# Fixed order for the last branch product and the gated merge of a decoder trunk, with one weight split per block

## Chip, core and metric

The kernel runs on one core of a Trainium2 chip. Its time is the device time of one execution in microseconds; several executions are measured and the median is given. Lower is better.

## What is computed

The reference is one layer of a hybrid decoder trunk over 1024 tokens of width 1024. Three branches (a linear recurrence, a stick-breaking attention and a cross-attention) each give 512 columns per token. The part that matters here joins them:

```
branch_out = einsum('btnc,ncd->btnd', ys, w_branch)
gates = sigmoid(gate_logits)
merged = sum(gates * branch_out, axis=2)
x = x + merged @ w_out
x = x + conv_ffn(x, norm2_g, w_up, conv_w, conv_b, w_down)
```

## The kernel before

Matrix products are made in split form. An operand x is kept as a high part, a rounded copy of x in a format that TensorE multiplies directly, and a low part, x minus that copy. A product is then three matmuls: high by high, high by low, low by high. Splitting takes two steps. For a weight, ScalarE makes the high part (L80) and POOL the low part (L81), both in `split_raw`; `load_w` (L76) issues the load on SP's queue into one of two buffers named wr. A buffer can be loaded again only when POOL has finished with it.

Two of the three branches are done and summed when `branch_last` (L1259) starts. It treats the remaining branch, branch 0, in eight blocks d of 128 output columns, each over all 1024 tokens. One load of branch weights (named wr, split into wh and wl) serves two blocks. For each block:

- SP loads the block's gate (L1270, into g, a tile of the pool "at") and the sum of the other two branches (L1271, into o, a tile of the pool "w4"). Three blocks of each fit.
- TensorE makes 24 matmuls of 128 rows by 512 columns (L115) into two PSUM banks, pp[0] and pp[1], one for each half of the tokens. There are four banks of this kind ("mm"), so that block d + 2 writes the banks of block d.
- VectorE multiplies the banks by the gate (L1286, one PSUM and one SBUF input) and adds the other branches' sum (L1287, two SBUF inputs).
- ScalarE makes the high part of the result (L1293: one piece of 512 columns, two of 256) and VectorE the low part (L1294, two SBUF inputs). These are the tiles mg of the projection.

Beside this the output weights are split. `load_wo` (L1254) does it for one of eight weights k. Weights 0 to 3 go into tiles "qk", 4 to 6 into tiles "at", 7 into "it" and "sp". In the program text four of them are asked for in `branch_last`, at blocks 2 to 5, and four at the head of `out_proj` (L1296). The projection multiplies tile by tile: in its first round, rows 0 and 1 of the tokens take turns, six matmuls each, for k from 0 to 7.

The program text doesn't fix the order on an engine. A scheduler places each instruction by its dependences and priorities, except those that are handed to `keep_in_program_order`, which keep their order on their engine. Matmuls in this part are not pinned, and neither were the splits, copies and merge steps.

Of the kernel before, what the change touches and what calls it, by code (L numbers as in the profile page):

```python
# [11 lines left out]
F32 = mybir.dt.float32  # L12
F32R = mybir.dt.float32r
BF16 = mybir.dt.bfloat16
AF = mybir.ActivationFunctionType
ALU = mybir.AluOpType
# [33 lines left out]
class Trunk:  # L50
# [25 lines left out]
        self.nc.sync.dma_start(raw, src)  # L76
        return raw

    def split_raw(self, raw, hi, lo):
        self.nc.scalar.activation(hi, raw, AF.Copy)  # L80
        self.nc.gpsimd.tensor_tensor(lo, raw, hi.bitcast(F32), ALU.subtract)  # L81
        return hi, lo

    def split_w(self, src):
        raw = self.load_w(src)
        hi = self.pool_wt.tile([128, 1024], F32R, name=self.nm("wh"), tag="wh", bufs=2)
        lo = self.pool_wt.tile([128, 1024], F32R, name=self.nm("wl"), tag="wl", bufs=2)
        return self.split_raw(raw, hi, lo)

    def mm3(self, outs, w, x, first, last):  # L90
        for pi, (a, b) in enumerate(((0, 0), (0, 1), (1, 0))):
# [1159 lines left out]
            items.append(self.branch_item(b, d, st, first))  # L1251
        return load, hooks, items

    def load_wo(self, k):  # L1254
        slots = ["qk"] * 8 + ["at"] * 6 + ["it", "sp"]
        hl = [self.pool_l.tile([128, 1024], F32R, name="wo_sp", tag="sp", bufs=1) if s == "sp" else self.t4(s, F32R) for s in slots[2 * k : 2 * k + 2]]
        self.wo.append(self.split_raw(self.load_w(self.I["w_out"][k]), *hl))

    def branch_last(self):  # L1259
        nc = self.nc  # L1260
        self.wo = []
        y = self.split_y(self.yT, True)
        mg = lambda name, shape: self.pool_l.tile(shape, F32R, name=name, tag="l4")
        self.mg0 = [[mg(f"mg0_{i}_{k}", [128, 2, 512]) for k in range(4)] for i in range(2)]
        self.mg1 = [[[mg(f"mg1_{i}_{t}_{k}", [128, 4, 256]) for k in range(2)] for t in range(2)] for i in range(2)]
        for d in range(8):
            if d % 2 == 0:
                w = self.split_w(self.I["w_br"][0, d // 2])
            g, o = self.t4("at"), self.t4()
            nc.sync.dma_start(g, self.gsd[0, d])  # L1270
            nc.sync.dma_start(o, self.mrd[d])  # L1271
            pp = [self.ps("mm"), self.ps("mm")]
            if d == 0:
                for i, (a, b) in enumerate(((0, 0), (1, 0), (0, 1))):
                    for k in range(4):
                        for h in range(2):
                            self.mmul(pp[h], w[a][:, k * 256 : k * 256 + 128], y[k][b][:, h * 512 : (h + 1) * 512],
                                      start=(i == 0 and k == 0), stop=(i == 2 and k == 3))
            else:
                for k in range(4):  # L1280
                    self.branch_mm(d, w, y, pp, k)
            if d in (2, 3, 4, 5):
                self.load_wo(d - 2)
            for h in range(2):
                hs = slice(h * 512, (h + 1) * 512)
                nc.vector.tensor_tensor(g[:, hs], pp[h], g[:, hs], ALU.mult)  # L1286
                nc.vector.tensor_tensor(g[:, hs], g[:, hs], o[:, hs], ALU.add)  # L1287
                if h == 0:
                    parts = [[self.mg0[i][d // 2][:, d % 2] for i in range(2)] + [slice(0, 512)]]
                else:  # L1290
                    parts = [[self.mg1[i][t][d // 4][:, d % 4] for i in range(2)] + [slice(512 + 256 * t, 768 + 256 * t)] for t in range(2)]
                for hi, lo, ts in parts:
                    nc.scalar.activation(hi, g[:, ts], AF.Copy)  # L1293
                    nc.vector.tensor_tensor(lo, g[:, ts], hi.bitcast(F32), ALU.subtract)  # L1294

    def out_proj(self):  # L1296
        nc = self.nc
# [738 lines left out]
```

## Time and profile before

| | us |
|---|---|
| median of 3 executions | 1805.65 (1805.49 to 1806.79) |
| the profiled execution | 1808.55 |
| its span, first to last instruction | 1806.8 |
| TensorE busy in the span | 1783.4 |
| VectorE, ScalarE, POOL busy | 1182.9, 864.3, 791.7 |
| first matmul of block 0 | at 1018.47 |
| first matmul of the projection | at 1064.80 |

Times in rows of a timeline are microseconds from the start of the span: start, duration, engine, line, operation, output and inputs, number of instructions that the row joins, and in brackets the idle time before it with what ended it. A row of waits gives who waited, for whom, the total, how often, and the longest. A row of a line's instructions gives the shortest, median and longest duration in ns. A row of loads ends with their size and the median time from issue to landing. A row of a window gives its length, then busy time and number of instructions of TensorE, its weight loads, VectorE, ScalarE and POOL, the granted TensorE clock, the DMA share and GB/s. PE is TensorE, PEld its weight loads, DVE VectorE, ACT ScalarE, POOL GpSimd, SP the engine whose queue issues most loads.

### The profile page before, as it was taken

What the parts mean: (1) busy time and instruction counts of PE and PEld (TensorE: products, weight loads), DVE (VectorE), ACT (ScalarE), POOL (GpSimd) and SP (SyncE); (2) the same over time, 40 slices, a digit from 0 to 9 for tenths busy, and PEclk for the clock granted to TensorE, in tenths of its full rate; (3) what the DMA queues carried; (4) which work ended last, traced back from release to release, by engine and by line L of the source; (5) the groups of instructions that cost most, each with busy time, mean ns of one, the idle gap of its engine ahead of it and who ended that gap; (6) DMA issues with size and microseconds to landing.
All of it is one profiled execution on the core that took longest, in us unless ns stands there. A gap on an engine that the chain in (4) does not pass through costs nothing.

```text
span 1806.8 us, 27325 instructions
## 1 busy us (share of the span) xinstructions
PE 1783.4 (99%) x10479; PEld 1446.0 (80%) x10479; DVE 1182.9 (65%) x1626; ACT 864.3 (48%) x1556; POOL 791.7 (44%) x448
## 2 busy tenths in 40 slices
PE   9999999999999999999999999989999999999999
PEld 7777778888888888777777878867888888888887
DVE  5667775898987534244443872577776777795596
ACT  6444344566566535534444334543544444454343
POOL 3223353322231462122333542486767767545454
PEclk9999999999999999999999999999999999999999
DMA  5255664211112352577654553222332323486476
GB/s 208 59 163 176 196 208 157 73 42 45 53 56 88 115 129 79 192 239 277 206 187 176 186 198 106 105 87 88 123 100 88 116 101 111 134 304 226 146 237 206
DMA packets 122772, 261.29 MB, mean 145 GB/s; under 512 B 28681, under 2 KB 43657, under 8 KB 122514
## 3 DMA queue, kind: packets, MB, share of 16 engines
q1 hardware_dynamic: 85026, 193.83, 32.7%
q10 hardware_dynamic: 33840, 53.10, 8.0%
q0 software_dynamic: 3776, 12.62, 2.3%
q8 instruction: 82, 1.34, 0.3%
q14 instruction: 48, 0.39, 0.1%
HBM read 178.99 MB, written 80.48 MB: 144 GB/s over the span
## 4 chain that ended last, share of the span: by engine, by line
PE 69%; DVE 7%; ACT 3%; issue 2%; POOL 2%; DMA 1%; SPq 0%; DVEq 0%; POOLq 0%; ACTq 0%
PE mm L115 57%; PE g L115 10%; PE g L105 2%; DVE at L926 1%; DVE it L545 1%; DMA wr<-in_w_out_dram 1%; DVE mg L1294 1%; POOL wl L81 1%; DVE inst L547 1%; DMA A<-yd 0%; ACT at L1143 0%; DVE w L821 0%; DVE at L1286 0%; DVE g L1530 0%; DVE at L1287 0%
## 5 line engine op out<-in xcount | busy, mean ns | idle before, releaser
L81 POOL TENSOR_TENSOR wl<-wr,wh 128x1024 fp32r<-128x1024 f32 (+2 forms) x78 | 195.9, 2512 | 501.5 <-ACT wh L80 492.0
L115 PE MATMUL mm<-xhi,wh 128*128 128x512 f32 x784 | 260.1, 413 | 0.5 <-DVE w L322 0.4
L115 PE MATMUL mm<-xlo,wh 128*128 128x512 f32 x784 | 243.5, 392 | 0.0
L115 PE MATMUL mm<-xhi,wl 128*128 128x512 f32 x784 | 242.5, 391 | 0.0
L115 PEld LDWEIGHTS mm<-xlo,wh 128*128 128x128 f32 x784 | 147.1, 188 | 33.2 <-DVE xlo L199 0.3
L115 PEld LDWEIGHTS mm<-xhi,wl 128*128 128x128 f32 x784 | 147.0, 188 | 33.0 <-POOL wl L81 0.7
L115 PEld LDWEIGHTS mm<-xhi,wh 128*128 128x128 f32 x784 | 136.7, 190 | 29.2 <-issue 6.1
L80 ACT ACTIVATE wh<-wr 128x1024 fp32r<-128x1024 f32 (+2 forms) x78 | 81.8, 1048 | 146.4 <-PE mm L115 93.3
L115 PE MATMUL mm<-dw,da 128*128 128x512 f32 x528 | 121.0, 390 | 0.0
L115 PE MATMUL mm<-BT,wh 128*128 128x512 f32 x352 | 111.8, 399 | 6.7 <-DVE u L1585 5.8
L115 PE MATMUL mm<-BT,l 128*128 128x512 f32 x504 | 117.6, 389 | 0.0
L115 PEld LDWEIGHTS mm<-dw,da 128*128 128x128 f32 x528 | 98.9, 188 | 21.5 <-DVE da L1746 1.0
L1747 POOL TENSOR_TENSOR dw<-draw,dw 128x512 fp32r<-128x512 f32 x55 | 81.9, 1497 | 77.3 <-ACT dw L1745 75.9
L926 DVE TENSOR_TENSOR_SCAN at<-at,nrt 128x128 f32<-128x128 f32 (+3 forms) x64 | 94.2, 1479 | 25.5 <-ACT at L920 25.3
L115 PEld LDWEIGHTS mm<-BT,l 128*128 128x128 f32 x504 | 94.6, 188 | 19.7
L115 PE MATMUL mm<-B,wh 128*128 128x512 f32 x352 | 108.6, 390 | 0.0
L1746 DVE TENSOR_TENSOR da<-draw,da 128x512 fp32r<-128x512 f32 x77 | 65.9, 862 | 53.2 <-ACT da L1744 52.9
L1465 POOL TENSOR_TENSOR l<-it,l 128x1024 fp32r<-128x1024 f32 x21 | 51.2, 2436 | 92.9 <-ACT l L1462 92.8
L115 PE MATMUL g<-dw,da 128*128 128x512 f32 x396 | 90.2, 389 | 0.0
L821 DVE TENSOR_TENSOR w<-w,nrt 128x1024 f32<-128x1024 f32 x24 | 49.9, 2078 | 58.1 <-ACT w L820 47.1
L115 PEld LDWEIGHTS g<-dw,da 128*128 128x128 f32 x396 | 74.3, 188 | 15.4
L1744 ACT ACTIVATE da<-draw 128x512 fp32r<-128x512 f32 x77 | 48.1, 627 | 80.4 <-PE mm L115 32.3
(335 smaller groups left out, 3990.9 us busy)
## 6 DMA issues: line engine op xcount, KB each, us to landing
wr<-in_w_in_dram SPq DMA_DIRECT2D x48, 512.0 KB, 3.6
draw<-actd SPq DMA_DIRECT2D x77, 256.0 KB, 3.3
draw<-in_w_down_dram SPq DMA_DIRECT2D x55, 256.0 KB, 4.5
at<-scr SPq DMA_DIRECT2D x24, 512.0 KB, 5.8
wr<-in_w_up_dram SPq DMA_DIRECT2D x22, 512.0 KB, 3.5
actd<-gall ACTq DMA_DIRECT2D x44, 256.0 KB, 3.3
rw<-in_w_up_dram SPq DMA_DIRECT2D x20, 512.0 KB, 3.7
gsd<-w ACTq DMA_DIRECT2D x18, 512.0 KB, 2.8
```

Of the source, the lines that this page charges most:

```text
L80: self.nc.scalar.activation(hi, raw, AF.Copy)
L81: self.nc.gpsimd.tensor_tensor(lo, raw, hi.bitcast(F32), ALU.subtract)
L105: self.pinned(self.nc.tensor.transpose(out, in_, self.ident[:n, :n]))
L115: self.pinned(self.nc.tensor.matmul(*a, **k))
L545: self.pinned(nc.vector.tensor_tensor(tv, X[:, 0:s, s : s + 1].to_broadcast([128, s, n]), X[:, s : s + 1, s + 1 : 64].to_broadcast([128, s ...
L547: self.pinned(nc.vector.tensor_tensor(X[:, 0:s, s + 1 : 64], X[:, 0:s, s + 1 : 64], tv, ALU.add))
L821: nc.vector.tensor_tensor(g, g, self.nrb, ALU.mult)
L926: self.pinned(nc.vector.tensor_tensor_scan(sn[:, :W][:, ::-1], sn[:, :W][:, ::-1], self.nrt[:, 1152 - W :][:, ::-1], 1.0, ALU.mult, ALU.max))
L1465: ins = nc.gpsimd.tensor_tensor(lo, src, hi.bitcast(F32), ALU.subtract)
L1744: self.pinned(nc.scalar.activation(A[:, 0], a, AF.Copy))
L1746: self.pinned(nc.vector.tensor_tensor(A[:, 1], a, A[:, 0].bitcast(F32), ALU.subtract))
L1747: nc.gpsimd.tensor_tensor(Wt[:, 1], w, Wt[:, 0].bitcast(F32), ALU.subtract)
```

## The change

`split_raw`, `split_w` and `load_wo` take an argument `fix`, which by default does nothing. In `branch_last` it is `keep_in_program_order`. The merge steps of VectorE and ScalarE are pinned with it, and so are the splits that the loop asks for. The first two branch weights and output weight 0 are asked for ahead of the loop, unpinned. In the loop each of blocks 0 to 4 asks for one split, behind its merge: output weight 1, branch weight 2, output weight 2, branch weight 3, output weight 3. In the text both multiplications now come ahead of both additions, and all subtractions behind the copies. Output weights 4 to 7 stay with the projection.

```diff
+        fix = self.tc.keep_in_program_order
+        ws = [self.split_w(self.I["w_br"][0, j]) for j in range(2)]
+        self.load_wo(0)
         for d in range(8):
-            if d % 2 == 0:
-                w = self.split_w(self.I["w_br"][0, d // 2])
+            w = ws[d // 2]
...
-            if d in (2, 3, 4, 5):
-                self.load_wo(d - 2)
+            halves = []
             for h in range(2):
                 hs = slice(h * 512, (h + 1) * 512)
-                nc.vector.tensor_tensor(g[:, hs], pp[h], g[:, hs], ALU.mult)
-                nc.vector.tensor_tensor(g[:, hs], g[:, hs], o[:, hs], ALU.add)
+                fix(nc.vector.tensor_tensor(g[:, hs], pp[h], g[:, hs], ALU.mult))
+            for h in range(2):
+                hs = slice(h * 512, (h + 1) * 512)
+                fix(nc.vector.tensor_tensor(g[:, hs], g[:, hs], o[:, hs], ALU.add))
...
                 for hi, lo, ts in parts:
-                    nc.scalar.activation(hi, g[:, ts], AF.Copy)
-                    nc.vector.tensor_tensor(lo, g[:, ts], hi.bitcast(F32), ALU.subtract)
+                    fix(nc.scalar.activation(hi, g[:, ts], AF.Copy))
+                    halves.append((lo, g[:, ts], hi.bitcast(F32)))
+            for lo, x, hi in halves:
+                fix(nc.vector.tensor_tensor(lo, x, hi, ALU.subtract))
+            if d in (1, 3):
+                ws.append(self.split_w(self.I["w_br"][0, d // 2 + 2], fix))
+            elif d in (0, 2, 4):
+                self.load_wo({0: 1, 2: 2, 4: 3}[d], fix)
```

What this makes of the engines' orders shows at three places. On ScalarE, from the last step ahead of the loop to the copies of block 1 (wr is a raw weight; wh a branch weight's and qk an output weight's high part; at a block's gate tile; mg its copies), the order before is:

```order
L80 ACTIVATE qk_9574<-wr_9576 128x1024
L820 ACTIVATE w_1457_9410<-mm_9360 128x512
L820 ACTIVATE w_1457_9410<-mm_9361 128x512
L80 ACTIVATE wh_9540<-wr_9538 128x1024
L824 ACTIVATE w_1457_9410<-w_1457_9410 128x1024
L826 DMA gsd<-w_1457_9410 128x1024
L80 ACTIVATE qk_9620<-wr_9622 128x1024
L1293 ACTIVATE mg_0_0_9436<-at_9458 128x512
L1293 ACTIVATE mg_0_0_0_9444<-at_9458 128x256
L1293 ACTIVATE mg_0_1_0_9446<-at_9458 128x256
L80 ACTIVATE wh_9638<-wr_9636 128x1024
L1293 ACTIVATE mg_0_0_9436<-at_9498 128x512
```

The same place on ScalarE in the changed kernel (its L1296 is the L1293 of before):

```order
L80 ACTIVATE qk_9464<-wr_9466 128x1024
L80 ACTIVATE wh_9460<-wr_9458 128x1024
L820 ACTIVATE w_1457_9410<-mm_9360 128x512
L820 ACTIVATE w_1457_9410<-mm_9361 128x512
L824 ACTIVATE w_1457_9410<-w_1457_9410 128x1024
L826 DMA gsd<-w_1457_9410 128x1024
L1296 ACTIVATE mg_0_0_9436<-at_9470 128x512
L1296 ACTIVATE mg_0_0_0_9444<-at_9470 128x256
L1296 ACTIVATE mg_0_1_0_9446<-at_9470 128x256
L80 ACTIVATE qk_9510<-wr_9512 128x1024
L1296 ACTIVATE mg_0_0_9436<-at_9516 128x512
```

The split of branch weight 1 has moved ahead of L820, and the split of output weight 1 from ahead of block 0's copies to behind them; between two blocks' copies there is now one split. On POOL, the low parts of the splits during the loop stood so before (qk and at belong to output weights, wl to branch weights):

```order
L81 TENSOR_TENSOR qk_9575<-wr_9576,qk_9574 128x1024
L81 TENSOR_TENSOR wl_9541<-wr_9538,wh_9540 128x1024
L81 TENSOR_TENSOR qk_9621<-wr_9622,qk_9620 128x1024
L81 TENSOR_TENSOR wl_9639<-wr_9636,wh_9638 128x1024
L81 TENSOR_TENSOR qk_9673<-wr_9674,qk_9672 128x1024
L81 TENSOR_TENSOR qk_9719<-wr_9720,qk_9718 128x1024
L81 TENSOR_TENSOR wl_9737<-wr_9734,wh_9736 128x1024
L81 TENSOR_TENSOR at_9821<-wr_9822,at_9820 128x1024
```

The same splits on POOL in the changed kernel:

```order
L81 TENSOR_TENSOR qk_9465<-wr_9466,qk_9464 128x1024
L81 TENSOR_TENSOR wl_9461<-wr_9458,wh_9460 128x1024
L81 TENSOR_TENSOR qk_9511<-wr_9512,qk_9510 128x1024
L81 TENSOR_TENSOR wl_9559<-wr_9556,wh_9558 128x1024
L81 TENSOR_TENSOR qk_9603<-wr_9604,qk_9602 128x1024
L81 TENSOR_TENSOR wl_9651<-wr_9648,wh_9650 128x1024
L81 TENSOR_TENSOR qk_9695<-wr_9696,qk_9694 128x1024
L81 TENSOR_TENSOR at_9821<-wr_9822,at_9820 128x1024
```

Output and branch weights now alternate throughout; branch weight 3 (wl_9737 before, wl_9651 now) has moved ahead of output weight 3. On SP, the queue of loads at the loop's start (gsd are the stored gates, mrd the stored sums of the other branches) was before:

```order
L1270 DMA at_9458<-gsd 128x1024
L1270 DMA at_9498<-gsd 128x1024
L1270 DMA at_9544<-gsd 128x1024
L76 DMA wr_9576<-in_w_out_dram 128x1024
L1271 DMA w_1470_9459<-mrd 128x1024
L1271 DMA w_1474_9499<-mrd 128x1024
L76 DMA wr_9622<-in_w_out_dram 128x1024
L76 DMA wr_9636<-in_w_br_dram 128x1024
```

The same place on SP in the changed kernel:

```order
L1272 DMA at_9470<-gsd 128x1024
L76 DMA wr_9466<-in_w_out_dram 128x1024
L1272 DMA at_9516<-gsd 128x1024
L1272 DMA at_9562<-gsd 128x1024
L76 DMA wr_9512<-in_w_out_dram 128x1024
L1273 DMA w_1476_9471<-mrd 128x1024
L1273 DMA w_1483_9517<-mrd 128x1024
L76 DMA wr_9556<-in_w_br_dram 128x1024
```

Output weight 0's load has moved ahead of the gates of blocks 1 and 2, and output weight 1's load, which waits for POOL, ahead of the sums of blocks 0 and 1. The orders of TensorE and VectorE are the same in both kernels.

More of the change, by code (lines that the diff above doesn't have):

```diff
@@ L77, in load_w, with split_raw, split_w @@
         return raw
-    def split_raw(self, raw, hi, lo):
-        self.nc.scalar.activation(hi, raw, AF.Copy)
-        self.nc.gpsimd.tensor_tensor(lo, raw, hi.bitcast(F32), ALU.subtract)
+    def split_raw(self, raw, hi, lo, fix=lambda ins: ins):
+        fix(self.nc.scalar.activation(hi, raw, AF.Copy))
+        fix(self.nc.gpsimd.tensor_tensor(lo, raw, hi.bitcast(F32), ALU.subtract))
         return hi, lo
-    def split_w(self, src):
+    def split_w(self, src, fix=lambda ins: ins):
         raw = self.load_w(src)
@@ L87, in split_w @@
         lo = self.pool_wt.tile([128, 1024], F32R, name=self.nm("wl"), tag="wl", bufs=2)
-        return self.split_raw(raw, hi, lo)
+        return self.split_raw(raw, hi, lo, fix)
     def mm3(self, outs, w, x, first, last):
@@ L1252, in branch, with load_wo @@
         return load, hooks, items
-    def load_wo(self, k):
+    def load_wo(self, k, fix=lambda ins: ins):
         slots = ["qk"] * 8 + ["at"] * 6 + ["it", "sp"]
         hl = [self.pool_l.tile([128, 1024], F32R, name="wo_sp", tag="sp", bufs=1) if s == "sp" else self.t4(s, F32R) for s in slots[2 * k : 2 * k + 2]]
-        self.wo.append(self.split_raw(self.load_w(self.I["w_out"][k]), *hl))
+        self.wo.append(self.split_raw(self.load_w(self.I["w_out"][k]), *hl, fix))
     def branch_last(self):
```

## Prediction

> **What bounds the kernel now.** I read the page first, then the waits and the timelines of the stretch from 1018 to 1078 us, where the changed loop runs. The page:
>
> ```profile
> span 1806.8 us, 27325 instructions
> PE 1783.4 (99%) x10479; PEld 1446.0 (80%) x10479; DVE 1182.9 (65%) x1626; ACT 864.3 (48%) x1556; POOL 791.7 (44%) x448
> ```
>
> TensorE is the bound, so the change can only bring what TensorE loses in this stretch. The waits name one cause:
>
> ```profile
> PEld mm L115 <- DVE at L1286: 4.5, 7, 1.1
> PE mm L115 <- DVE at L1286: 1.6, 3, 0.6
> ```
>
> L1286 is the multiply that empties a pair of PSUM banks. With four "mm" banks, block d+2 cannot start before L1286 of block d is done. TensorE's timeline gives the loss:
>
> ```profile
> 1018.47 1.98 PE L115 MATMUL mm<-at,wh 128*128 128x512 f32 x8
> ...
> 1023.91 0.62 PE L115 MATMUL mm<-at,wh 128*128 128x512 f32 x2
> ...
> 1034.33 0.61 PE L115 MATMUL mm<-at,wl 128*128 128x512 f32 x2
> 1035.53 1.09 PE L115 MATMUL mm<-at,wh 128*128 128x512 f32 x2 [0.59 <-DVE at L1286]
> ...
> 1047.49 1.10 PE L115 MATMUL mm<-at,wh 128*128 128x512 f32 x2 [0.39 <-DVE at L1286]
> ...
> 1053.47 1.00 PE L115 MATMUL mm<-at,wh 128*128 128x512 f32 x2
> ...
> 1064.80 1.52 PE L115 MATMUL mm<-qk,mg 128*128 128x512 f32 x6
> 1066.96 10.19 PE L115 MATMUL mm<-qk,mg 128*128 128x512 f32 x42 [0.64 <-DVE at L1286]
> 1076.99 8.32 PE L115 MATMUL mm<-at,mg 128*128 128x512 f32 x36
> ```
>
> Block 0 takes 1023.91 - 1018.47 = 5.44 us for 24 matmuls, 0.2267 us each. Eight blocks and the first six matmuls of the projection are 198 matmuls, so an unhindered TensorE is at 1018.47 + 198 x 0.2267 = 1063.35. It gets on at 1066.96, 3.6 us late. After a stop the first matmuls are slow as well: the 42 from 1066.96 take 10.03 us to the next row instead of 42 x 0.2267 = 9.52, which adds 0.5. The loss is 4.1 us, and that is the ceiling of the gain here. It falls at block 3 (1035.53), block 5 (1047.49), block 6 (the 1.00 in place of 0.62) and the second row of the projection (1066.96).
>
> Why L1286 is late stands in the other timelines, VectorE, POOL, ScalarE:
>
> ```profile
> 1024.06 1.28 DVE L1286 TENSOR_TENSOR at<-mm,at 128x512 f32<-128x512 f32 x2
> ...
> 1029.53 5.34 DVE L1294 TENSOR_TENSOR mg<-at,mg 128x512 fp32r<-128x512 f32 x3 [1.98 <-ACT mg L1293]
> 1034.80 1.28 DVE L1286 TENSOR_TENSOR at<-mm,at 128x512 f32<-128x512 f32 x2
> ...
> 1037.38 1.36 DVE L1294 TENSOR_TENSOR mg<-at,mg 128x512 fp32r<-128x512 f32 x3
> ...
> 1047.95 1.28 DVE L1287 TENSOR_TENSOR at<-at,w 128x512 f32<-128x512 f32 x2
> ...
> 1061.55 3.48 DVE L1287 TENSOR_TENSOR at<-at,w 128x512 f32<-128x512 f32 x2
> ...
> 1066.23 1.28 DVE L1286 TENSOR_TENSOR at<-mm,at 128x512 f32<-128x512 f32 x2
> ```
>
> ```profile
> 1029.06 2.40 POOL L81 TENSOR_TENSOR qk<-wr,qk 128x1024 fp32r<-128x1024 f32 x1 [2.65 <-ACT qk L80]
> 1032.01 2.58 POOL L81 TENSOR_TENSOR wl<-wr,wh 128x1024 fp32r<-128x1024 f32 x1 [0.56 <-ACT wh L80]
> ...
> 1061.61 2.88 POOL L81 TENSOR_TENSOR at<-wr,at 128x1024 fp32r<-128x1024 f32 x1 [10.11 <-ACT at L80]
> ```
>
> ```profile
> 1019.51 1.06 ACT L80 ACTIVATE qk<-wr 128x1024 fp32r<-128x1024 f32 x1 [7.54 <-DMA wr<-in_w_out_dram]
> 1020.48 1.07 ACT L820 ACTIVATE w<-mm 128x512 f32<-128x512 f32 x2
> ...
> 1027.92 1.06 ACT L80 ACTIVATE qk<-wr 128x1024 fp32r<-128x1024 f32 x1 [2.69 <-DMA wr<-in_w_out_dram]
> 1028.88 1.23 ACT L1293 ACTIVATE mg<-at 128x512 fp32r<-128x512 f32 x3
> ...
> 1048.66 1.33 ACT L1293 ACTIVATE mg<-at 128x512 fp32r<-128x512 f32 x3
> ...
> 1060.47 1.06 ACT L80 ACTIVATE at<-wr 128x1024 fp32r<-128x1024 f32 x1 [0.73 <-DVE mg L1294]
> ```
>
> Two things are to be seen. First, in block 0 ScalarE stood at 1027.92 on a split whose load had not landed, with the merge's copies (L1293) behind it. Second, the merge's subtractions then met two splits on POOL, 1029.06 and 1032.01, and three that take 1.36 us at 1037.38 took 5.34. By line:
>
> ```profile
> L1286 DVE TENSOR_TENSOR at<-mm,at x16: 675/680/686, 1024.1 to 1066.8; 128x512 f32<-128x512 f32 x16
> L1294 DVE TENSOR_TENSOR mg<-at,mg x24: 410/420/2712, 1029.5 to 1073.4; 128x256 fp32r<-128x256 f32 x16, 128x512 fp32r<-128x512 f32 x8
> L81 POOL TENSOR_TENSOR qk<-wr,qk x4: 2388/2540/2837, 1020.7 to 1043.4; 128x1024 fp32r<-128x1024 f32 x4
> ```
>
> L1286, which reads PSUM, never varies; L1294, with both inputs in SBUF, is 420 ns or over 2 us. So POOL's split and a VectorE operation on two SBUF tiles exclude each other for a whole instruction. That fits: the pair from 1061.55 ends at 1065.03, 0.54 us after the split from 1061.61 (2.88 long) ends at 1064.49, the length of the one half that waited.
>
> **The change, part by part.** No instruction is added or removed. VectorE's order stays (L1286 twice, L1287 twice, L1294 three times per block was its order already), as does TensorE's, so those two lines of the edit cost nothing and give nothing. What moves are splits on ScalarE and POOL and loads on SP.
>
> *One split per block.* Let T be the end of L1287's second half. Copies L1293 end at T + 0.76 (1049.99 against 1049.23, from the rows at 1048.66 and 1047.95). The split's first half takes 1.06, POOL starts 0.08 later (1061.61 against 1061.53) and takes 2.39 alone. Then both halves of the next L1287 end 0.56 + 0.60 = 1.16 after POOL. Sum 5.45 per block, as long as TensorE's 5.44. L1294 (1.36) and the next L1286 (1.28) fit in the 3.5 us in which ScalarE and POOL do the split: POOL arrives at T + 1.9, when L1294 is over and L1286, which isn't held up, is running. That cover is what the fixed order buys. Were it gone (split and subtractions colliding), a block would take up to 2.39 more.
>
> *Start of the chain.* The issue of the first output weight's load, and the median landings of this stretch:
>
> ```profile
> 1013.18 0.33 SPq L76 DMA_DIRECT2D wr<-in_w_out_dram x1
> ```
>
> ```profile
> wr<-in_w_out_dram SPq DMA_DIRECT2D x8, 512.0 KB, 4.6
> w<-mrd SPq DMA_DIRECT2D x8, 512.0 KB, 4.4
> ...
> at<-in_w_up_dram SPq DMA_DIRECT2D x1, 512.0 KB, 3.5
> ```
>
> The load still goes out at 1013.18 (POOL frees its buffer then), but with two gate loads behind it instead of ahead. It took 6.3 us (to 1019.51); at the median 4.6 it lands at 1017.8. Bounds are the 3.5 us of a load that ran alone and the 6.3. Its split ends on ScalarE at 1018.9, that of branch weight 1 at 1019.9, L820 at 1021.0 against 1021.55. POOL ends the first split at 1021.3, or 0.9 later if it meets a VectorE operation first, as it may at this place. Only then does SP issue the second output weight and, new behind it, the sum of block 0 (L1271): landing 0.4 + 4.4 later, at 1026.1 to 1027.0. That is the first cost of the change, since L1287 of block 0 ran from 1025.26 before; now it begins with that landing, and its two halves (1.2) end at T0 = 1027.3 to 1028.2. The two gate loads that moved behind the weight go out 1 to 3 us later, and the first is needed when block 1 ends, 1018.47 + 2 x 5.44 = 1029.3: nothing.
>
> *End of the chain.* T5 = T0 + 5 x 5.45 = 1054.5 to 1055.5, L1294 of block 5 ends 1.45 later. The next split (output weight 4) must wait for it, because its buffer is block 5's gate tile (the 0.73 at 1060.47), so POOL is done 1.06 + 0.08 + 2.39 later, 1059.5 to 1060.5. L1287 of block 6 ends 0.56 to 1.16 after that, L1294 1.45 later, and L1286's first half of block 7 0.68 after that: 1062.7 to 1063.8, TensorE's own end of block 7 (1061.99) included. TensorE wants those banks at 1063.35. Earlier banks are free in time: L1286 of block 3 ends 2.7 us after T2, by 1041.8, and block 5 starts at 1018.47 + 5 x 5.44 = 1045.7. The remaining stall is 0 to 0.5, and any stall costs 0.5 of slow start too. I take 0.5 + 0.5 = 1.0 of the 4.1, near the late end because every term is a free duration. Far bounds: 0 lost, or all 4.1, with L1286 of block 7 where it was (1066.23).
>
> *Weights for TensorE.* Branch weights 2 and 3 are now split behind output weights. By the chain their second halves are ready at T1 + 5.45 - 1.16 = 1037.0 to 1037.9 and two blocks later, 1047.9 to 1048.8. TensorE needs them 0.9 us into blocks 4 and 6: 1018.47 + 4 x 5.44 + 0.9 = 1041.1 and 1052.0. Three microseconds are in hand: nothing. The last four output weights follow as before; the first of them is done at 1060.5 and is needed four steps of twelve matmuls into the projection, 1061.99 + 4 x 2.72 = 1072.9.
>
> *What follows.* From 1067 the chain lies on TensorE, and its next waits are on results that come from the same projection:
>
> ```profile
> 1067.56 25.92 PE mm L115 x113
> PE mm L115 <- DVE u L1585: 5.8, 2, 3.6
> ```
>
> So the gain passes through. Sum: 4.1 - 1.0 = 3.1 us. The profiled execution took 1808.55 us (span 1806.8, 1.75 around it), 2.9 above the median 1805.65; I take the same 3.1 off the median: 1802.6.
>
> The Trainium skill, page "SBUF — State Buffer", section "A bandwidth-pool intuition that's wrong", describes the same exclusive lock but puts about 115 ns on a hand-over (measured there for DMA descriptors). By that figure, an estimate, two hand-overs in each of six blocks would take 1.4 us back, 1804.0; the 0.54 above shows none.
>
> **The rivals.** *Chain longer than 5.45.* If ScalarE's pick-up or a collision costs 0.2 to 0.6 us per block, the end of the chain comes 1 to 3 us later and the gain is 0.1 to 2: 1803.6 to 1805.6, middle 1804.6. For it: real splits took 2540 ns in the middle, not 2388. Against: those met VectorE.
>
> *Slower: a late load in ScalarE's fixed order.* Output weight 2 is issued when POOL has finished weight 1 (about 1032.5), behind loads that wait for older results, and its split stands between the copies of blocks 2 and 3. At 4.6 us it lands at 1037.1 for a start at T2 + 0.8 = 1039. Later than that every microsecond delays the whole chain, and the end has no slack: 3.1 us more eats the gain, 6.7 more gives 1809.3. It takes a landing of 13 us, twice the 6.3 above.
>
> *Clock.* The granted clock fell here:
>
> ```profile
> 1190.00:1200.00 10.00, 6.36 (x28) 5.00 (x27) 7.89 (x12) 5.67 (x9) 8.79 (x7) 0.92 0.36 105
> 1200.00:1210.00 10.00, 10.00 (x34) 7.96 (x34) 5.28 (x9) 5.63 (x8) 9.84 (x7) 0.74 0.18 52
> ```
>
> It follows the 3.6 us wait on L1585, and 26% of 10 us is 2.6 us lost. If the shift spares this loss, the time is 1802.6 - 2.6 = 1800.0. The row shows that it happened once, not how it depends on the moment. The Trainium skill, "TensorE: Matmul & The Clock Gate", section "The HAM clock gate", says that the gate looks at free-running windows of 3413 ns; by it, whether a 3.6 us gap costs clock is a matter of phase, in either kernel.
>
> *It does nothing.* VectorE's order is unchanged; if the late L1286 came from elsewhere, 1805.6, the end of the first rival.
>
> **How the numbers follow.** 0.2%, 3.6 us, is about what a measurement of this kernel can tell from no change, and the forecast lies just inside. Forecast 0.62 (gain 2.0 to 4.1): 0.24 of it over 3.6, 0.38 under. First rival, with nothing gained, 0.20: same. Clock 0.10: faster. Slower 0.08. Sums: faster 0.34, same 0.58, slower 0.08. The range leaves out the slower rival and about the clock's 0.10: from 1801.2 (the 4.1, and 0.35 of the spread between runs) to 1805.7.
>
> **Right or wrong.** Right: no TensorE wait on L1286 before the projection's second row, there at most 0.5 us; L1287 about every 5.45 us; one POOL split per block, over before the next L1287 starts; nothing of L1294 over 1 us until block 6. Wrong: TensorE waits on a weight's split in blocks 4 or 6, ScalarE on a load between copies, or L1287 of block 0 ends after 1029.

## The result, and the profile after

The changed kernel takes **1801.48 us** (median of 11 runs, 1799.33 to 1804.63) against 1805.65 for the kernel before (11 runs beside it, 1803.08 to 1808.66): ratio 0.9978, 95% interval 0.9970 to 0.9987, that is 2.3 to 5.4 us less. Measured once more beside the kernel before on another chip, the ratio was 0.9974 (0.9965 to 0.9984). One execution of the kernel before in that second measurement took 3570.88 us, a slow run, and the ratios are of fast runs alone. So the changed kernel is faster by a little over 0.2%. The profiled execution took 1801.44 us:

```profile
span 1799.7 us, 27322 instructions
PE 1777.5 (99%) x10479; PEld 1444.2 (80%) x10479; DVE 1177.3 (65%) x1626; ACT 864.1 (48%) x1556; POOL 789.0 (44%) x448
```

TensorE does the same 10479 matmuls in 5.9 us less busy time, since a matmul that starts late or runs slowly, at a lower clock too, counts as busy here. The line numbers have moved: the multiply L1286 is now L1287, the add L1287 is L1290, the copy L1293 is L1296, the subtraction L1294 is L1299, and L1585 is L1594. TensorE's timeline in the loop and the projection's first round:

```profile
1017.00 1.98 PE L115 MATMUL mm<-at,wh 128*128 128x512 f32 x8
...
1060.52 11.32 PE L115 MATMUL mm<-qk,mg 128*128 128x512 f32 x48
1071.68 8.32 PE L115 MATMUL mm<-at,mg 128*128 128x512 f32 x36
...
1082.56 5.61 PE L115 MATMUL mm<-qk,mg 128*128 128x512 f32 x24
```

Block 0 starts 1.47 us earlier than before (1017.00 against 1018.47), for a reason outside this loop that is taken up further down; times from here on are compared after adding 1.47. From block 0 to the projection TensorE has no gap: 1060.52 - 1017.00 = 43.52 us for 192 matmuls, 0.2267 each, the unhindered pace of before. From the first matmul of block 0 to the first of the projection's second round lie 288 matmuls, 65.29 us at that pace. What is over 65.29 is the loss, and the measure used from here on. Changed kernel: 1082.56 - 1017.00 = 65.56, a loss of **0.27 us**. Before, by the same count in its trace (1018.47 to 1087.87): 69.40, a loss of **4.11 us**. The difference is 3.84 us, of the 4.17 between the medians. The rest of the loss sits in the 48 matmuls of the row at 1060.52, 11.32 long.

VectorE's timeline, around block 0, in the middle and at the end:

```profile
1020.50 3.42 DVE L821 TENSOR_TENSOR w<-w,nrt 128x1024 f32<-128x1024 f32 x1
1023.84 1.27 DVE L1287 TENSOR_TENSOR at<-mm,at 128x512 f32<-128x512 f32 x2
1025.04 1.28 DVE L1290 TENSOR_TENSOR at<-at,w 128x512 f32<-128x512 f32 x2
...
1034.50 2.49 DVE L1290 TENSOR_TENSOR at<-at,w 128x512 f32<-128x512 f32 x2
1037.08 1.36 DVE L1299 TENSOR_TENSOR mg<-at,mg 128x512 fp32r<-128x512 f32 x3
1038.73 1.29 DVE L1287 TENSOR_TENSOR at<-mm,at 128x512 f32<-128x512 f32 x2 [0.28 <-PE mm L115]
...
1055.06 1.29 DVE L1287 TENSOR_TENSOR at<-mm,at 128x512 f32<-128x512 f32 x2 [0.59 <-PE mm L115]
1056.26 3.48 DVE L1290 TENSOR_TENSOR at<-at,w 128x512 f32<-128x512 f32 x2
...
1060.94 1.28 DVE L1287 TENSOR_TENSOR at<-mm,at 128x512 f32<-128x512 f32 x2
```

The three subtractions take 1.36 us, where before those of block 0 took 5.34. It is the adds (L1290) that meet POOL now: 2.49 and 3.48 in place of 1.28. And in the loop the multiply waits for TensorE (0.28, 0.59), no longer TensorE for the multiply. POOL, then ScalarE:

```profile
1019.46 3.38 POOL L81 TENSOR_TENSOR wl<-wr,wh 128x1024 fp32r<-128x1024 f32 x1
...
1033.44 2.40 POOL L81 TENSOR_TENSOR wl<-wr,wh 128x1024 fp32r<-128x1024 f32 x1 [2.94 <-ACT wh L80]
1038.78 2.40 POOL L81 TENSOR_TENSOR qk<-wr,qk 128x1024 fp32r<-128x1024 f32 x1 [2.94 <-ACT qk L80]
...
1056.74 2.46 POOL L81 TENSOR_TENSOR at<-wr,at 128x1024 fp32r<-128x1024 f32 x1 [4.88 <-PE mm L115]
```

```profile
1036.42 1.33 ACT L1296 ACTIVATE mg<-at 128x512 fp32r<-128x512 f32 x3 [3.06 <-DVE at L1290]
1037.65 1.05 ACT L80 ACTIVATE qk<-wr 128x1024 fp32r<-128x1024 f32 x1
```

There is one split per block, 5.34 us apart, and what ScalarE's copies wait for last is an add, never a load.

### The profile page after: what moved, and what is told of

Its sections match the earlier page's. It is cut to its first block, busy times and chain, and to the rows that moved or that the text cites. A ratio compares the mean times of both kernels' runs of the same rounds, so it can differ in the third digit from the quotient of the medians.

```text
span 1799.7 us, 27322 instructions
## 1 busy us (share of the span) xinstructions
PE 1777.5 (99%) x10479; PEld 1444.2 (80%) x10479; DVE 1177.3 (65%) x1626; ACT 864.1 (48%) x1556; POOL 789.0 (44%) x448
## 4 chain that ended last, share of the span: by engine, by line
PE 73%; DVE 5%; ACT 2%; issue 1%; POOL 1%; DMA 1%; DVEq 0%; POOLq 0%; ACTq 0%
PE mm L115 61%; PE g L115 10%; PE g L105 3%; DVE at L926 1%; DVE it L545 1%; DMA A<-yd 1%; DVE inst L547 0%; ACT at L1143 0%; DVE w L821 0%; DVE g L1539 0%; DVE qk L866 0%; DVE g L1540 0%; DVE qk L865 0%; POOL wl L81 0%; POOL l L1474 0%
## 5 line engine op out<-in xcount | busy, mean ns | idle before, releaser
L1755 DVE TENSOR_TENSOR da<-draw,da 128x512 fp32r<-128x512 f32 x77 | 61.5, 803 | 53.4 <-ACT da L1753 53.2
L821 DVE TENSOR_TENSOR w<-w,nrt 128x1024 f32<-128x1024 f32 x24 | 50.6, 2110 | 56.3 <-ACT w L820 45.4
```

The costliest lines, as they stand in the source:

```text
L821: nc.vector.tensor_tensor(g, g, self.nrb, ALU.mult)
L1755: self.pinned(nc.vector.tensor_tensor(A[:, 1], a, A[:, 0].bitcast(F32), ALU.subtract))
```

## The experiments

Three theories were to be told apart. **Lock**: the loss came from VectorE's operations on two SBUF tiles that met POOL's splits at the wrong place, and the place of the splits is what the change mends. **Load**: it came from ScalarE standing on late loads in front of the copies. **Form**: pins, or the new order of VectorE's text, bring the gain by themselves. The losses of TensorE, worked out as above (first matmul of block 0, first matmul of the projection's second round, in us):

| kernel | from | to | loss |
|---|---|---|---|
| before | 1018.47 | 1087.87 | 4.11 |
| changed | 1017.00 | 1082.56 | 0.27 |
| e8, before with short subtractions on POOL | 1017.04 | 1082.67 | 0.34 |
| e5, before with fills in place of subtractions | 1018.85 | 1084.12 | 0.0 |
| e1, changed without pins | 1018.82 | 1089.28 | 5.17 |
| e2, pins on the old text | 1016.87 | 1119.24 | 37.1 |
| e9, changed, halves in turn | 1018.85 | 1100.49 | 16.4 |
| e3, splits ahead of the merge | 1017.73 | 1083.31 | 0.29 |
| e4, two splits in one gap | 1017.16 | 1084.06 | 1.61 |
| e6, a quarter of a split more | 1017.18 | 1082.76 | 0.29 |
| e7, a whole low half more | 1019.04 | 1085.98 | 1.65 |
| e10, weight 4's split behind block 6 | 1017.49 | 1082.77 | 0.0 |

### e8: POOL's lock cut short, the loads left as they were

```diff
-        self.wo.append(self.split_raw(self.load_w(self.I["w_out"][k]), *hl))
+        hi, lo = hl
+        raw = self.load_w(self.I["w_out"][k])
+        self.nc.scalar.activation(hi, raw, AF.Copy)
+        self.nc.gpsimd.memset(lo[:, 64:].bitcast(F32), 0.0)
+        self.nc.gpsimd.tensor_tensor(lo[:, :64], raw[:, :64], hi[:, :64].bitcast(F32), ALU.subtract)
+        self.wo.append(hl)
```

> The kernel before, with the orders of ScalarE and SP as they were, but POOL subtracts only the first 64 columns of each output weight's low half and fills the other 960 with zeros; this leaves out the low part of 960 of the 1024 columns of these weights. The load buffers are still held until POOL has read them, so ScalarE still stands on late loads in front of copies. Theory (the meeting of POOL's long subtractions with VectorE's operations on two SBUF tiles is needed for the loss): TensorE's loss in the loop and the projection's first rows falls from 3.9 us to under 0.5. Rival (ScalarE's waits for late loads are enough): 2 us or more of loss stay.

One run, 1804.81 us (the kernel before beside it: 1808.21). ScalarE still stands on loads in front of copies; two of these waits:

```profile
1026.27 1.06 ACT L1259 ACTIVATE qk<-wr 128x1024 fp32r<-128x1024 f32 x1 [3.38 <-DMA wr<-in_w_out_dram]
...
1044.12 1.06 ACT L80 ACTIVATE wh<-wr 128x1024 fp32r<-128x1024 f32 x1 [4.26 <-DMA wr<-in_w_br_dram]
```

TensorE's only late matmul in the loop is the start of block 6, two matmuls in 0.78 us to the next row in place of 0.45:

```profile
1049.68 0.94 PE L115 MATMUL mm<-at,wh 128*128 128x512 f32 x2
1050.46 0.62 PE L115 MATMUL mm<-A,wh 128*128 128x512 f32 x2
```

The loss is 0.34: with the same orders on ScalarE and SP and waits on loads of 3.38 and 4.26 us, 3.8 of the 4.1 us are gone. The copies are no earlier for it: block 0's start 2.03 us behind the end of their adds (1027.23 against 1025.20), where before it was 1.32 (1028.88 against 1027.56). So Lock holds, and Load alone is worth 0.34 at most. Even this rest has a lock in it: in front of the late matmul the subtractions of block 3 meet the split of a branch weight, which e8 leaves whole. VectorE's row, then POOL's:

```profile
1045.73 3.14 DVE L1299 TENSOR_TENSOR mg<-at,mg 128x512 fp32r<-128x512 f32 x3 [2.69 <-ACT mg L1298]
```

```profile
1045.25 2.40 POOL L81 TENSOR_TENSOR wl<-wr,wh 128x1024 fp32r<-128x1024 f32 x1 [6.13 <-ACT wh L80]
```

### e5: the same, with fills only

```diff
-        self.wo.append(self.split_raw(self.load_w(self.I["w_out"][k]), *hl))
+        self.nc.scalar.activation(hl[0], self.load_w(self.I["w_out"][k]), AF.Copy)
+        self.nc.gpsimd.memset(hl[1].bitcast(F32), 0.0)
+        self.wo.append(hl)
```

> The kernel before, but POOL fills the low halves of all eight output weights with zeros in place of the subtraction; this leaves out the low part of these weights, and frees their load buffers when ScalarE has read them. Theory (the loss before comes from VectorE operations on two SBUF tiles that meet POOL's subtractions): the loss of TensorE in the loop and the projection's first rows falls from 4 us to under 1, the only long L1294 stand beside the branch weights' splits. Rival (the loss comes from ScalarE standing on late loads in front of the copies, or from the halves' order): over 2 us of loss stays.

One run, 1803.31 us (before beside it: 1807.51); no loss. Alone it would prove less than e8, since the load buffers come free earlier here. What it adds is one fill of POOL and one pair of adds at the same moment, VectorE's row first:

```profile
1058.10 1.28 DVE L1289 TENSOR_TENSOR at<-at,w 128x512 f32<-128x512 f32 x2
```

```profile
1058.51 0.95 POOL L1258 MEMSET at<- 128x1024 f32 x1 [10.91 <-PE mm L115]
```

Neither holds up the other (1.28 is the free time of the pair). The Trainium skill, page "SBUF — State Buffer", section "SBUF: two separate sides", says that VectorE's operations with two SBUF inputs meet only GpSimd operations that read SBUF; these rows agree.

### e1: the new text without the pins

```diff
-        fix = self.tc.keep_in_program_order
+        fix = lambda ins: ins
```

> The changed kernel's text without the pins: VectorE's and TensorE's orders stay as changed; on ScalarE the split of output weight 1 falls back ahead of L824 and block 0's copies, and two splits together fall between the copies of blocks 0 and 1 and of blocks 2 and 3. Theory (what counts is one split in each gap between copies, behind the block's own copies): subtractions meet POOL's splits again (over 2 us for some), TensorE waits again for the multiply that empties the banks, 2 to 4 us in the loop and the projection's first rows, time 1804 to 1806. Rival (the new order of the text and the early branch weights are enough): no TensorE gap in the loop, time as the changed kernel, 1801.5.

Median of 12 runs 1806.08 us, ratio to before 0.9994 (0.9986 to 1.0003): the whole gain is gone. The loss, 5.17, is more than the 2 to 4 expected, and nearly all of it falls at the start of block 6. ScalarE, then POOL, VectorE and TensorE:

```profile
1046.76 1.06 ACT L80 ACTIVATE qk<-wr 128x1024 fp32r<-128x1024 f32 x1 [4.33 <-DMA wr<-in_w_out_dram]
1047.72 1.04 ACT L80 ACTIVATE wh<-wr 128x1024 fp32r<-128x1024 f32 x1
1048.67 1.23 ACT L1296 ACTIVATE mg<-at 128x512 fp32r<-128x512 f32 x3
```

```profile
1047.89 2.41 POOL L81 TENSOR_TENSOR qk<-wr,qk 128x1024 fp32r<-128x1024 f32 x1 [9.25 <-ACT qk L80]
1050.25 2.81 POOL L81 TENSOR_TENSOR wl<-wr,wh 128x1024 fp32r<-128x1024 f32 x1
```

```profile
1049.32 4.37 DVE L1299 TENSOR_TENSOR mg<-at,mg 128x512 fp32r<-128x512 f32 x3 [3.80 <-ACT mg L1296]
1053.61 1.28 DVE L1287 TENSOR_TENSOR at<-mm,at 128x512 f32<-128x512 f32 x2
```

```profile
1054.43 1.30 PE L115 MATMUL mm<-at,wh 128*128 128x512 f32 x2 [2.81 <-DVE at L1287]
1055.53 1.05 PE L115 MATMUL mm<-A,wh 128*128 128x512 f32 x2
```

A late load puts two splits together ahead of the copies of block 3, the subtractions (4.37 for 1.36) meet both on POOL, and the multiply behind them frees block 6's banks 2.8 us late. After the stop pairs of matmuls take 0.85 us to the next row in place of 0.45. Here the late load (4.33 us of waiting) and the lock (3.0 us of longer subtractions) both add to the delay, and this run does not separate them; e8 does. The order of the text alone is worth nothing: Form falls in its first half.

### e2 and e9: what the pins need

e2 puts the pins on the old text, e9 keeps everything of the change but the order of the halves. The edits, e2 first:

```diff
-        ws = [self.split_w(self.I["w_br"][0, j]) for j in range(2)]
-        self.load_wo(0)
         for d in range(8):
-            w = ws[d // 2]
+            if d % 2 == 0:
+                w = self.split_w(self.I["w_br"][0, d // 2], fix)
...
-            halves = []
+            if d in (2, 3, 4, 5):
+                self.load_wo(d - 2, fix)
             for h in range(2):
                 hs = slice(h * 512, (h + 1) * 512)
                 fix(nc.vector.tensor_tensor(g[:, hs], pp[h], g[:, hs], ALU.mult))
-            for h in range(2):
-                hs = slice(h * 512, (h + 1) * 512)
                 fix(nc.vector.tensor_tensor(g[:, hs], g[:, hs], o[:, hs], ALU.add))
...
-                    halves.append((lo, g[:, ts], hi.bitcast(F32)))
-            for lo, x, hi in halves:
-                fix(nc.vector.tensor_tensor(lo, x, hi, ALU.subtract))
-            if d in (1, 3):
-                ws.append(self.split_w(self.I["w_br"][0, d // 2 + 2], fix))
-            elif d in (0, 2, 4):
-                self.load_wo({0: 1, 2: 2, 4: 3}[d], fix)
+                    fix(nc.vector.tensor_tensor(lo, g[:, ts], hi.bitcast(F32), ALU.subtract))
```

```diff
-            halves = []
             for h in range(2):
                 hs = slice(h * 512, (h + 1) * 512)
                 fix(nc.vector.tensor_tensor(g[:, hs], pp[h], g[:, hs], ALU.mult))
-            for h in range(2):
-                hs = slice(h * 512, (h + 1) * 512)
                 fix(nc.vector.tensor_tensor(g[:, hs], g[:, hs], o[:, hs], ALU.add))
...
-                    halves.append((lo, g[:, ts], hi.bitcast(F32)))
-            for lo, x, hi in halves:
-                fix(nc.vector.tensor_tensor(lo, x, hi, ALU.subtract))
+                    fix(nc.vector.tensor_tensor(lo, g[:, ts], hi.bitcast(F32), ALU.subtract))
```

> The pins alone, put on the old order of the text: each half of a block in turn goes through multiply, add, copy, subtract, and blocks 2 and 4 have two splits in one gap. Theory (the gain comes from the order, that is from subtractions behind all copies and one split per gap): VectorE waits for ScalarE's copies between the halves and for splits in front of these copies; TensorE loses 5 to 15 us in the loop, time 1808 to 1816. Rival (pinning as such, against the scheduler, brings the gain): time 1801 to 1803.

> The changed kernel with all its early weights, pins and splits, but each half of a block in turn through multiply, add, copy and subtract on VectorE and ScalarE. Theory (the long waits of the pins alone came from branch weights pinned behind the merge of the block before; the halves' order is a second, smaller cost): no wait of TensorE on a branch weight; VectorE stands 0.7 and 0.5 us per block on copies, so a block takes at least 5.3 us and with POOL's split 6 to 7; TensorE loses 3 to 8 us on the multiply that empties the banks. Rival (the halves' order costs nothing as long as the splits are where they are): TensorE loses under 0.5 us as in the changed kernel.

e2: median of 4 runs 1837.28 us, ratio 1.0171 (1.0158 to 1.0184). It is slower, but its loss of 37.1 us is more than twice the 15 that the forecast allowed for, and the reason is mainly one that the forecast did not name. TensorE's waits from 1015 to 1110, and ScalarE's rows at block 2:

```profile
PE mm L115 <- ACT wh L80: 21.0, 3, 7.7
PE mm L115 <- DVE at L1287: 4.2, 2, 2.4
PE mm L115 <- POOL wl L81: 1.1, 3, 0.4
```

```profile
1031.89 0.72 ACT L1294 ACTIVATE mg<-at 128x256 fp32r<-128x256 f32 x2 [2.08 <-DVE at L1288]
1032.52 1.04 ACT L80 ACTIVATE wh<-wr 128x1024 fp32r<-128x1024 f32 x1
```

The split of block 2's branch weight, asked for at block 2, is pinned behind block 1's copies; TensorE wants it as soon as block 1 is multiplied. Three times TensorE waits for the weight of the block that it is to start, 21.0 us. The changed kernel asks for branch weights two blocks ahead, which by itself looks like nothing and is what the pins rest on.

e9: one run, 1818.7 us, loss 16.4, no wait for a branch weight, as forecast; but 3 to 8 was the forecast. VectorE's rows of one block:

```profile
1039.27 2.85 DVE L1287 TENSOR_TENSOR at<-at,w 128x512 f32<-128x512 f32 x1
1042.82 0.69 DVE L1294 TENSOR_TENSOR mg<-at,mg 128x512 fp32r<-128x512 f32 x1 [0.70 <-ACT mg L1293]
...
1045.32 0.76 DVE L1294 TENSOR_TENSOR mg<-at,mg 128x256 fp32r<-128x256 f32 x2 [0.48 <-ACT mg L1293]
...
1046.71 2.85 DVE L1287 TENSOR_TENSOR at<-at,w 128x512 f32<-128x512 f32 x1
```

A block takes 1046.71 - 1039.27 = 7.44 us, 2.0 more than TensorE's 5.44, over five blocks and then the projection's rows. VectorE waits for ScalarE's copies of the same block (0.70, 0.48), and since copies and split follow each other on ScalarE, the add of the next block always meets the whole split. So both halves of Form fall: pins without early weights, and pins without the halves put together, are slower than before.

### e3 and e4: where the splits stand

e3 asks for each split ahead of its block's merge in place of behind it:

```diff
+            if d in (1, 3):
+                ws.append(self.split_w(self.I["w_br"][0, d // 2 + 2], fix))
+            elif d in (0, 2, 4):
+                self.load_wo({0: 1, 2: 2, 4: 3}[d], fix)
             halves = []
...
-            if d in (1, 3):
-                ws.append(self.split_w(self.I["w_br"][0, d // 2 + 2], fix))
-            elif d in (0, 2, 4):
-                self.load_wo({0: 1, 2: 2, 4: 3}[d], fix)
```

e4 asks for two behind block 1, two behind block 3 and one behind block 4:

```diff
             if d in (1, 3):
                 ws.append(self.split_w(self.I["w_br"][0, d // 2 + 2], fix))
-            elif d in (0, 2, 4):
-                self.load_wo({0: 1, 2: 2, 4: 3}[d], fix)
+                self.load_wo(d // 2 + 1, fix)
+            elif d == 4:
+                self.load_wo(3, fix)
```

> The changed kernel, with each split asked for ahead of its block's merge in place of behind it; still one split per gap, but all one gap earlier (output weight 1 ahead of block 0's copies). Theory (one split per gap counts, the exact gap does not): block 0's sum is 1 to 2 us later through one collision with POOL, the chain's period stays 5.3 to 5.5, TensorE loses less than 0.6 us in the loop, time within 0.8 of the changed kernel's. Rival (that the split stands behind the copies counts): TensorE loses 1 to 3 us, time 1802.5 to 1804.5.

> The changed kernel with two splits (a branch weight and an output weight) behind block 1, two behind block 3, one behind block 4, none behind blocks 0 and 2. Theory (each gap with two splits makes the chain longer by about a split's share that the gaps without one give back only in part): the last merges are about 2 us late, TensorE waits about 1.5 to 2 us at the projection's second row and loses 0.5 more in slow start; no stall earlier than block 5. Rival (any pinned order between copies is as good): no gap in TensorE from block 0 to the projection's end.

e3: loss 0.29, the changed kernel's within 0.02. Its median of 12 runs is 1803.27, ratio 0.9984 (0.9975 to 0.9992). That is 1.8 us above the changed kernel's median from another measurement, not within the 0.8 forecast; the intervals overlap, and the trace shows nothing in this part that would make a difference.

e4: one run, 1803.11 us. No stall before block 5 nor in the loop at all, one at the second row:

```profile
1060.68 1.52 PE L115 MATMUL mm<-qk,mg 128*128 128x512 f32 x6
1063.16 10.19 PE L115 MATMUL mm<-qk,mg 128*128 128x512 f32 x42 [0.95 <-DVE at L1287]
```

The loss is 1.61 (1.5 to 2 of waiting and 0.5 after it were expected): two splits in one gap cost 1.3 us even in a pinned order, of which a wait for a load ahead of one split (0.36 at 1050.48) is a quarter at most. In these traces it does not matter in which gap a single split stands; that it is single does.

### e6 and e7: how much is in hand

A part of output weight 3's low half is made twice on POOL, 256 columns in e6, all 1024 in e7 (there the last line has 1024 in place of 256):

```diff
-    def load_wo(self, k, fix=lambda ins: ins):
+    def load_wo(self, k, fix=lambda ins: ins, again=0):
...
-        self.wo.append(self.split_raw(self.load_w(self.I["w_out"][k]), *hl, fix))
+        raw = self.load_w(self.I["w_out"][k])
+        self.wo.append(self.split_raw(raw, *hl, fix))
+        if again:
+            fix(self.nc.gpsimd.tensor_tensor(hl[1][:, :again], raw[:, :again], hl[0][:, :again].bitcast(F32), ALU.subtract))
...
-                self.load_wo({0: 1, 2: 2, 4: 3}[d], fix)
+                self.load_wo({0: 1, 2: 2, 4: 3}[d], fix, 256 * (d == 4))
```

> The changed kernel, with 256 of the 1024 columns of output weight 3's low half made twice on POOL (about 0.6 us more, same values). The chain of merges has 0.26 us in hand at block 7's first multiply. Theory (POOL's splits are on the chain that sets this multiply): TensorE waits 0.2 to 0.5 us at the projection's second row, and about 0.5 us of slow start behind it. Rival (the chain is not on the path, or has more cover): no gap.

> The changed kernel, with the whole low half of output weight 3 made twice on POOL (about 2.4 us more, same values). Theory (POOL's splits are on the chain, 0.26 us in hand): TensorE waits 1.8 to 2.4 us at the projection's second row, and about 0.5 us of slow start behind it. Rival (the chain is not on the path, or has more cover): no gap or one under 1 us.

e6: one run, 1802.07 us, loss 0.29, nothing more than the changed kernel's. POOL's extra operation and VectorE's multiply of block 6:

```profile
1052.12 1.07 POOL L1260 TENSOR_TENSOR qk<-wr,qk 128x256 fp32r<-128x256 f32 x1
```

```profile
1055.23 1.29 DVE L1290 TENSOR_TENSOR at<-mm,at 128x512 f32<-128x512 f32 x2 [0.22 <-PE mm L115]
```

The theory of 0.26 us in hand falls: VectorE's wait for TensorE at this place shrank from 0.59 to 0.22, and that took it up. e7: one run, 1804.76 us, TensorE waits 0.99 at the second row, loss 1.65, which is 1.38 over the changed kernel's and not the 2.3 to 2.9 expected. In e7's trace block 5's subtractions come 2.06 us later (1057.20 - 1019.04 against 1053.10 - 1017.00), of which 0.69 are taken up ahead of block 6's multiply, most of it the 0.59 of waiting: 1.37 are left. So POOL is on the path, with 0.7 in hand, more than forecast.

### e10: the last 0.27 us, and the repeat

The changed kernel's rest sits at block 7's multiply, behind the adds of block 6 that meet output weight 4's split (3.48 above). Pinned behind block 6's merge, that split meets other work:

```diff
+            elif d == 6:
+                self.load_wo(4, fix)
...
-        for k in range(4, 8):
+        for k in range(5, 8):
```

> The changed kernel with output weight 4's split pinned behind block 6's merge in place of ahead of it. Theory (the 0.28 us that TensorE still loses at the second matmul of the projection's second row come from the add of block 6 that meets this split): block 6's two adds take 1.28 in place of 3.48 us, block 7's multiply starts when TensorE is done with its block, no loss at the second row, and none later. Rival (this cost is set elsewhere, or comes back when weight 4 is late): 0.28 us or more stay.

```profile
1056.75 1.29 DVE L1290 TENSOR_TENSOR at<-at,w 128x512 f32<-128x512 f32 x2
```

```profile
1061.01 11.04 PE L115 MATMUL mm<-qk,mg 128*128 128x512 f32 x48
```

The adds are free again, the 48 matmuls take 11.04 in place of 11.32, and the loss is nil. Both kernels were then timed side by side:

> The changed kernel once more, beside the kernel before on another chip. By the trace of the loop and the projection's first rows it gains 3.8 us, a ratio of 0.9979; theory: the ratio's interval holds 0.9979 and not 1. Rival (more or less is gained elsewhere, by the clock or at the projection's end): the interval lies apart from 0.9979.

> The changed kernel with output weight 4's split pinned behind block 6, timed. The trace gives it 0.28 us over the changed kernel, 0.016%; theory: a median within 1 us of the changed kernel's in the same call, not to be told apart. Rival (it costs later, since the weights 5 to 7 come later): over 1 us slower.

Changed kernel 1801.16 us, ratio 0.9974 (0.9965 to 0.9984); with weight 4 moved 1801.99, ratio 0.9979 (0.9968 to 0.9991). The trace's 3.84 us, a ratio of 0.9979, lies in both intervals. The traces of these two repeats give the same losses again: 0.28 (1018.92 to 1084.49) and nil (1016.72 to 1082.00). The 0.28 us is seen in the traces alone; no time here can tell it.

## Why the prediction was right

**Ceiling.** 4.1 us was read off the rows of before, 4.11 is its loss by count, and e8 shows the lock to be its cause. Right.

**What stays.** This is the term that was mis-sized: 1.0 us was taken, 0.27 came. The multiply's first half of block 7 ended at 1060.94 + 0.68 + 1.47 = 1063.09, inside the forecast 1062.7 to 1063.8 and 0.26 before TensorE wants it. The prediction looked at the first half only; the small stall is at the second matmul of the row, which writes the other bank. That bank came free at 1060.94 + 1.28 + 1.47 = 1063.69, and TensorE wanted it at 1063.35 + 0.23 = 1063.58. A short stall brought hardly any slow start: 0.5 had been taken over from the longer stop of before. These 0.73 us are most of the 1.1 between the forecast 1802.6 and 1801.48.

**The chain.** 5.45 us per block was worked out, 5.34 measured (POOL's rows at 1033.44 and 1038.78). Every piece is as given but one: the split's first half starts at 1037.65, 0.10 before the copies' row ends at 1037.75, while the sum had put them end to end. By the hand-over of 115 ns that the prediction cited from the Trainium skill ("SBUF — State Buffer", "A bandwidth-pool intuition that's wrong") a block would take 0.23 more than the sum, an estimate; the rows show none of it.

**The chain's start: the right number for a wrong reason.** The adds of block 0 were forecast to begin at 1026.1 to 1027.0, because their sum is loaded late; they began at 1025.04 + 1.47 = 1026.51. But no load was waited for: the row has no wait, and the load had landed at 1024.32. What was late was VectorE: L821 took 3.42 us (2.56 before), held by the split of branch weight 1 on POOL (1019.46, 3.38 long), which the change had moved ahead of it. The prediction counted that move on ScalarE's side (L820 at 1021.0) and missed it on VectorE's.

**The chain's end.** Output weight 4's split was put behind block 5's gate tile alone. It started on POOL at 1056.74, with TensorE as its releaser, and was done at 1059.20 + 1.47 = 1060.67, past the forecast 1059.5 to 1060.5. That it hangs on TensorE and not only on the chain fits e6, which cost nothing: there this split starts 39.73 us behind block 0, here 39.74.

**Weights.** Low halves of branch weights 2 and 3 were due at 1037.0 to 1037.9 and 1047.9 to 1048.8; they ended at 1033.44 + 2.40 + 1.47 = 1037.31 and, with the row at 1044.11 (2.40 as well), at 1047.98. Right.

**What follows.** The wait on the up projection's operand stayed (L1585 before 5.8 us in two, 3.6 the longest):

```profile
PE mm L115 <- DVE u L1594: 5.7, 2, 3.6
```

So the gain passes through. The two profiled executions differ by more, 1808.55 - 1801.44 = 7.1 us. The clock is the rest, in two places. Before, one window ahead of the loop:

```profile
620.00:630.00 10.00, 7.72 (x69) 7.29 (x69) 0.14 (x1) 3.92 (x8) 7.41 (x5) 0.83 0.67 205
```

After, the same window and the one behind the longest wait:

```profile
620.00:630.00 10.00, 7.72 (x88) 7.22 (x87) 0.11 (x1) 3.99 (x9) 7.91 (x5) 1.00 0.70 210
...
1190.00:1200.00 10.00, 6.36 (x21) 4.78 (x20) 6.78 (x12) 3.87 (x5) 9.84 (x7) 0.83 0.16 55
...
1210.00:1220.00 10.00, 7.98 (x28) 6.09 (x28) 8.37 (x10) 2.25 (x3) 9.06 (x5) 0.83 0.34 131
```

17% of 10 us, 1.7, was lost ahead of the loop before and not after: there is the 1.47. Behind the wait on L1594 1.7 us are lost, where before 0.8 and 2.6 were: 1.7 less. The 1.7 lost from 1210 to 1220 has its like before, from 1220 to 1230 (0.83 there too), and makes no difference. 3.84 + 1.47 + 1.7 make 7.0 of the 7.1.

Neither of these losses follows the change in the traces at hand. The window ahead of the loop has 0.83 in the traces of before, e1, e5, e7, e9 and the changed kernel's own repeat, where block 0 starts at 1018.47 to 1019.04, and 1.00 in all the others, where it starts at 1016.72 to 1017.73. The repeat also lost 3.4 us behind the wait (0.74 and 0.92 in the windows from 1190 and 1200), as much as before.

**Signs.** Two did not hold to the letter. Each POOL split was to be over before the next L1287 starts, but the split from 1033.44 ends at 1035.84, and the adds behind it had started at 1034.50 and took 2.49; that they wait for POOL and end 1.15 behind it is what the chain's own sum says. And ScalarE did wait for a load between copies, 1.40 us at 1062.86 between those of blocks 6 and 7; it cost nothing, since block 7's copies behind it still waited 0.60 for their add.

**Rivals.** A longer chain: no, it was shorter. A late load in ScalarE's fixed order: no, the copies always waited for an add last; e1 shows a harmful wait for a load, but with the scheduler's order. Clock: the profiled execution did lose less, but 1.7 us of it lay ahead of the changed code, and the repeat lost as much as before. Whether the change moves these slow windows on average stays open; the ratios do not need it, since 3.84 us alone lies in both intervals. That it does nothing: refuted by e1 and e8.

## What to carry to other kernels

Where POOL and VectorE work on SBUF side by side, look for the one operation per loop pass that may be held up for a whole POOL instruction, and put POOL's work there, once per pass; e4 and e1 show what two in one gap cost. A pin fixes all that stands behind the pinned instruction too: whatever another engine needs next must be asked for passes ahead, or the pin turns into a wait of the bound engine (e2). Slack is read at every wait of the chain, not at its end: in e6 the cover was VectorE's 0.59 us of waiting a block earlier.

## What the hardware showed that had not been expected

POOL is held up as well: a subtraction of 64 columns took 0.32 us alone and 0.87 at 1036.81, beside adds that had started at 1036.21 (e8); 256 columns took 1.07 beside adds (e6). A fill of 128x1024 on POOL and a pair of adds on VectorE ran at their free 0.95 and 1.28 side by side (e5). After a stop of 2.8 us pairs of matmuls took 0.85 us and more for over 3 us (e1), at a granted clock of 0.50 (1055 to 1058). The first pairs behind the short stops of before took 0.94 to the next row at a granted clock of 1.00 (1035 to 1037 and 1047 to 1049), so that slow start is no loss of clock; what it is stays open. After a hesitation of 0.15 at the second row of the changed kernel the loss was 0.27 in all. The losses of clock come in steps: 1.7 us in the window ahead of the loop before, 1.7 behind L1594 after, 3.4 (0.8 and 2.6) there before, which at half clock (0.50 in each microsecond from 625 to 628 before) are stretches of 3.4 and 6.8 us. The Trainium skill, "TensorE: Matmul & The Clock Gate", "The HAM clock gate", gives windows of 3413 ns, free-running; one and two such windows fit these steps.
